# A two-layer hybrid block (attention, convolution, Fourier) on one core: the Fourier gate's projection moved beside attention, and the first scale and shift used piece by piece for eight token tiles

## The chip, the core and the metric

The kernel runs on one core of a Trainium2 chip. The metric is the device time of one execution in microseconds (us). Before the change three runs gave a median of 1203.3 us (1202.12 to 1205.43).

## The reference, cut to what matters

Two layers over 1024 latent and 256 context tokens of width 1024. Each layer: a norm with scale and shift that come from a conditioning vector (adaLN), one wide projection whose columns feed three branches and their gates, and an output projection over the gated branches.

```python
for l in range(2):
    shift, scale, gate = split(silu(c) @ w_ada[l] + b_ada[l])        # and the same with c_ctx
    hc = rms_norm(h_ctx, norm_g[l]) * (1 + scale_c) + shift_c        # context
    hx = rms_norm(x, norm_g[l]) * (1 + scale) + shift                # latent
    # columns: q 512, k 128, v 128, g_att 512, c_a 256, c_b 256, g_conv 256, f_u 256, g_four 256
    px = split_cols(hx @ w_in[l])
    attn = windowed_attention(rope(q), rope(k), v, kc, vc, sink)     # +-128 tokens, and all of the context
    y_conv = silu(layer_norm(depthwise_conv31(c_a * sigmoid(c_b))))
    y_four = Re(fft2(f_u)) @ w_four + b_four
    y = concat([attn * silu(g_att), y_conv * silu(g_conv), y_four * silu(g_four)]) @ w_out[l]
    x = x + gate * y       # in layer 0 the context stream goes the same way
return rms_norm(x, final_g)
```

In layer 1 the context only gives keys and values.

## The kernel before

**Precision.** Every float32 matmul operand is held as two parts, hi and lo (`hxh`, `hxl` for the modulated input, `wh`, `wl` for weights), and each product is three matmuls (`mm3`, lines 195 to 197 in the profile). One column tile of the projection (128 columns, `C_GF`, `C_Q` and so on name the first) over one chunk of tokens is 8 blocks of the inner width times 3, so 24 matmuls into one PSUM bank. Layer 0 has three chunks (512 and 512 latent, 256 context), layer 1 two, and three for the keys and values.

**Order of the work.** The program is recorded call by call. A scheduler then places the instructions of each engine in a fixed order, by its own simulated timeline and a priority number that rises as the program is recorded (`tc.cur_priority`). So the order in which the code calls things shapes the order on each engine, without setting it alone. On the chip each engine runs its list in order and waits at semaphores.

**Startup.** `load_x` fetches a tile of 128 tokens; `first_norm` divides it by its root mean square (VectorE and GpSimd in turn). The scale and shift columns of layer 0 come in four pieces `u` of two column blocks each: `ada_load` (4 transfers of 512 KB), `ada_sums` (line 285, matmuls over `wada`), `ada_cols` (line 300, selector matmuls, then four small VectorE operations). `transposes` (line 380) turns normed tokens, and `modulate` (lines 393 and 396) applies scale and shift and makes `hxh` and `hxl`. `Pair` projects two column tiles, those of the Fourier input, chunk by chunk: `p0` for tokens 0 to 511, which follows the pieces; `p1` for tokens 512 to 1023; `p2` for the context.

**A layer.** The *projection stage* runs through `todo` by `projections`, a chunk at a time into the banks `mm` and `pt` in turn (`mmx`): both convolution inputs, then the two tiles of the Fourier gate (`C_GF`), keys, values, queries. Between chunks it advances `side()` (the Fourier transform `four`, gate rows, layer 1's scale and shift) and `fill_v(budget)`, which records some of the 31 taps of the convolution (`conv_taps`) on VectorE, as a background that `Behind` keeps behind other work. The gate of `C_GF` is finished by `gf_evac`: a tanh on ScalarE (line 514) and two products on VectorE (`t<-t,mm`, then `F<-F,t`).

*Attention* follows: `Attention`, 40 steps in layer 0 and 32 in layer 1, each for one block of 128 queries and two heads: scores (lines 893 and 895), softmax on VectorE, ScalarE and GpSimd, transposes (949), values (963). Between two steps PE is given one chunk from `rest()`: the attention gate (`C_GATT`), `conv_norm` (576, 594), the convolution gate (`C_GC`), then halves of the output projection (`OP`). The kernel's tail is the last output tiles and the final norm.

## Time and profile before

| what | value |
| --- | --- |
| median of 3 runs | 1203.3 us |
| the profiled execution | 1202.68 us, its span 1200.6 us |
| mean granted TensorE clock | 0.964 of full speed |
| TensorE (PE) busy | 1103.3 us, 92% of the span |
| VectorE (DVE) busy | 820.6 us, 68% |
| ScalarE (ACT) busy | 554.7 us, 46% |
| GpSimd (POOL) busy | 295.0 us, 25% |
| chain that ended last | PE 70%, DVE 10%, DMA 9%, ACT 4% |

The span is the time from the first to the last instruction that the profiler saw; 2.08 us of the execution lie outside it. Busy shares are means over stages with different limits: PE is nearly full in both projection stages, and has gaps in the startup, in both attentions and in the tail.

### The profile page before, as it was taken

The page shows a single profiled execution, that of the slowest core. Times are in us where ns is not written, and L with a number is a line of the kernel's source. Part 1 is how long each engine was busy: PE and PEld are TensorE (multiplying, and loading weights), DVE is VectorE, ACT ScalarE, POOL GpSimd, SP SyncE. Part 2 cuts the span into 40 slices and gives each one's busy share as a digit, 9 for nine tenths or more (in the row PEclk, how much of TensorE's full clock was granted, in tenths as well). Part 3 has the DMA queues.
Part 4 walks back from the last instruction along what each step waited for, and adds up shares of the span by engine and source line. Part 5 has one row for each costly group of instructions (what it writes and reads, how often), then busy time and mean ns, then how long its engine had stood idle before and what let it go on. Part 6 is the DMA issues. An engine that isn't in the chain of part 4 may idle for free.

```text
span 1200.6 us, 17131 instructions
## 1 busy us (share of the span) xinstructions
PE 1103.3 (92%) x6165; PEld 925.9 (77%) x6165; DVE 820.6 (68%) x1665; ACT 554.7 (46%) x1209; POOL 295.0 (25%) x266
## 2 busy tenths in 40 slices
PE   5799999999999989999889999999989979988866
PEld 3488887888888878888668788788778868877754
DVE  3425879999577786666755369889656786766654
ACT  5563222312566655564646652222255654545541
POOL 1212000000222443544342120000022453334321
PEclk9799999999999999999979999999989989999889
DMA  9602273744332433544436423532243453322221
GB/s 332 218 25 71 70 239 113 225 137 108 84 97 75 149 115 102 166 142 132 115 120 227 145 65 116 184 110 79 88 93 106 136 145 103 110 74 71 71 71 53
DMA packets 154093, 146.49 MB, mean 122 GB/s; under 512 B 7398, under 2 KB 131734, under 8 KB 154008
## 3 DMA queue, kind: packets, MB, share of 16 engines
q1 hardware_dynamic: 154008, 145.40, 39.5%
q8 instruction: 49, 0.80, 0.3%
q14 instruction: 36, 0.29, 0.1%
HBM read 110.49 MB, written 34.87 MB: 121 GB/s over the span
## 4 chain that ended last, share of the span: by engine, by line
PE 70%; DVE 10%; DMA 9%; ACT 4%; issue 3%; SPq 2%; POOL 1%; DVEq 0%; ACTq 0%; POOLq 0%
PE mm L195 13%; PE mm L197 13%; PE mm L196 13%; PE pt L195 5%; PE pt L196 5%; PE pt L197 5%; PE mm L963 4%; PE pt L949 4%; DMA od<-ot 3%; PE score L893 2%; DVE score L57 2%; DVE pl L57 2%; PE score L895 2%; DMA wr<-od 1%; ACT p L919 1%
## 5 line engine op out<-in xcount | busy, mean ns | idle before, releaser
L195 PE MATMUL mm<-hxh,wh 128*128 128x512 f32 (+1 forms) x808 | 311.5, 386 | 5.5 <-DVE t L57 3.2
L197 PE MATMUL mm<-hxh,wl 128*128 128x512 f32 (+1 forms) x808 | 306.7, 380 | 2.4 <-POOL wl L405 2.3
L196 PE MATMUL mm<-hxl,wh 128*128 128x512 f32 (+1 forms) x808 | 307.4, 380 | 0.0
L195 PEld LDWEIGHTS mm<-hxh,wh 128*128 128x128 f32 x808 | 153.8, 190 | 37.5 <-DVE t L57 4.3
L57 DVE SCALAR_TENSOR_TENSOR cy<-cu,cw,cy 128x1014 f32<-128x1014 f32 (+20 forms) x180 | 180.1, 1007 | 2.6
L197 PEld LDWEIGHTS mm<-hxh,wl 128*128 128x128 f32 x808 | 153.6, 190 | 30.3 <-POOL wl L405 3.1
L935 POOL TENSOR_SCALAR p<-p,st 128x640 f32<-128x640 f32 (+2 forms) x144 | 114.4, 809 | 249.1 <-DVE st L57 129.1
L196 PEld LDWEIGHTS mm<-hxl,wh 128*128 128x128 f32 x808 | 154.0, 191 | 25.0 <-issue 0.5
L405 POOL TENSOR_TENSOR wl<-wr,wh 128x1024 fp32r<-128x1024 f32 x26 | 64.2, 2468 | 396.3 <-ACT wh L404 394.1
L954 ACT ACTIVATE ph<-pt 128x512 fp32r<-128x512 f32 x184 | 97.4, 542 | 121.0 <-PE pt L949 118.2
L57 DVE TENSOR_TENSOR pl<-pt,ph 128x512 fp32r<-128x512 f32 x184 | 112.3, 616 | 57.8 <-ACT ph L954 56.4
L949 PE MATMUL pt<-ident,p 128*128 128x128 f32 x640 | 107.6, 286 | 24.5 <-DVE pl L57 19.1
L919 ACT ACTIVATE p<-score,st 128x640 f32<-128x640 f32 (+2 forms) x144 | 105.3, 734 | 36.5 <-DVE st L57 29.2
L57 DVE CUSTOM_DVE_ANT_0 score<-score,mask,nsink 128x640 f32<-128x640 f32 (+2 forms) x144 | 110.8, 782 | 13.8 <-PE score L895 13.0
L195 PE MATMUL pt<-hxh,wh 128*128 128x512 f32 (+1 forms) x296 | 112.2, 383 | 3.9 <-ACT hxh L393 2.5
L404 ACT ACTIVATE wh<-wr 128x1024 fp32r<-128x1024 f32 x56 | 59.7, 1066 | 116.5 <-PE mm L196 73.1
L196 PE MATMUL pt<-hxl,wh 128*128 128x512 f32 (+1 forms) x296 | 111.1, 376 | 0.7 <-DVE hxl L57 0.7
L197 PE MATMUL pt<-hxh,wl 128*128 128x512 f32 (+1 forms) x296 | 110.4, 373 | 0.9 <-DVE wl L57 0.9
L949 PEld LDWEIGHTS pt<-ident,p 128*128 128x128 f32 x640 | 79.8, 146 | 38.2 <-POOL p L935 8.7
L963 PE MATMUL mm<-ph,v 128*128 128x256 f32 x320 | 93.1, 314 | 13.2 <-ACT ph L954 10.7
L963 PE MATMUL mm<-pl,v 128*128 128x256 f32 x320 | 93.7, 315 | 5.3 <-DVE pl L57 4.9
L963 PEld LDWEIGHTS mm<-ph,v 128*128 128x128 f32 x320 | 64.6, 202 | 18.3 <-ACT ph L954 15.8
(220 smaller groups left out, 1797.8 us busy)
## 6 DMA issues: line engine op xcount, KB each, us to landing
wada<-w_ada SPq DMA_DIRECT2D x48, 512.0 KB, 7.0
wr<-w_in SPq DMA_DIRECT2D x38, 512.0 KB, 4.1
qq<-qd SPq DMA_DIRECT2D x36, 256.0 KB, 4.3
x1d<-x SPq DMA_DIRECT2D x10, 512.0 KB, 3.0
xnd<-xr SPq DMA_DIRECT2D x10, 512.0 KB, 3.7
p<-xnd SPq DMA_DIRECT2D x10, 512.0 KB, 4.8
sg<-sgd SPq DMA_DIRECT2D x36, 128.0 KB, 3.0
od<-ot SPq DMA_DIRECT2D x18, 256.0 KB, 2.5
```

Source lines behind the costliest of these rows:

```text
L57: r = f(*args, **kw)
L195: T.matmul(o, lhsT=lhs[0], rhs=rhs[0], start=start, stop=False)
L196: T.matmul(o, lhsT=lhs[0], rhs=rhs[1], start=False, stop=False)
L197: T.matmul(o, lhsT=lhs[1], rhs=rhs[0], start=False, stop=stop)
L404: S.activation(hi, raw, AF.Copy)
L405: (E or (G if holding[0] else V)).tensor_tensor(out=lo, in0=raw, in1=f32(hi), op=ALU.subtract)
L893: T.matmul(sc[:, c0:512], lhsT=q2[:, h, :], rhs=kx[:, k0:k0 + nl], start=fst, stop=not fst)
L919: S.activation(pp[:, j * n:(j + 1) * n], z["sc"][j][:, 768 - n:768], AF.Exp, scale=-1.0, bias=st[:, j:j + 1], accum_out=st[:, 4 + j:5 + j])
L935: G.tensor_scalar(out=pp[:, j * n:(j + 1) * n], in0=pp[:, j * n:(j + 1) * n], scalar1=st[:, 6 + j:7 + j], scalar2=1.0, op0=ALU.mult, op1=A ...
L949: T.transpose(out=bt[:, (j % 2 * 2 + y) * P:(j % 2 * 2 + y + 1) * P], in_=pp[:, c0:c0 + P], identity=ident)
L954: S.activation(ph, bt[:, :w], AF.Copy)
L963: T.matmul(o, lhsT=self.vv[kt][:, kv * P:(kv + 1) * P], rhs=y.cols(j * 256, (j + 1) * 256), start=(j == 0 and x == 0), stop=(j == z["nkt"] ...
```

## The change

It has five parts. First, the tiles of `C_GF` go from the projection stage to the front of attention's fillers, ahead of `C_GATT`, in the bank `mm`; the call that drained the Fourier transform inside `gf_evac` goes; the rope tables are loaded at the stage's third chunk; `side()` advances twice a chunk towards the stage's end; the budgets of taps rise from 3.0 and 5.0 to 4.0 and 6.0. Second, the taps are recorded with a priority number 300 higher, and in layer 0 the context's taps come ahead of the latent ones. Third, at the start each piece `u` of the scale and shift modulates tokens 0 to 511 and 512 to 1023 in turn, `p0` and `p1` advance step by step beside each other, and the loop that did `p1` afterwards goes. Fourth, for that the x tiles 4 to 7 are loaded ahead of the second piece of `wada`, and `ada_sums` and `ada_cols` use halves of a `score` bank. Fifth, in layer 0 `modulate` reads PSUM with one activation into `q`, and VectorE copies `q` to the hi part; before, two activations did that.

```diff
     def fill_v(us):
+        p0 = tc.cur_priority
+        tc.cur_priority = p0 + 300
         V.background = True
...
         V.background = False
+        tc.cur_priority = p0
...
             hi, lo = hx[k][0].cols(t0, t0 + n), hx[k][1].cols(t0, t0 + n)
-            for o in (hi, q):
+            for o in (q, hi)[:1 if l == 0 else 2]:
                 S.activation(o, two[:, j * n:(j + 1) * n], AF.Identity, scale=ada_col(1, st, k),
                              bias=ada_col(0, st, k))
+            if l == 0:
+                V.tensor_copy(out=hi, in_=q)
             E = G if k % 4 == 3 else V
...
                                    in1=z.cols(o0, o1), op0=ALU.mult, op1=ALU.add)
-        for s0, s1 in spans:
+        for s0, s1 in spans[::-1]:
             us = 1.25 if s0 == 0 else 0.4
...
                     back.append((us, lambda a=(s0, s1, j): tap(*a)))
-        back.append((0.0, u.put))
+            back.append((0.0, u.put_ctx if s0 else u.put_lat))
...
     wa = w_begin(0, C_FU)
-    z[1] = ada_load(1)
     first_norm(groups[0], (V, G))
...
     wb = w_tile_short(0, C_FU + P)
+    for t in groups[1]:
+        load_x(t)
+    z[1] = ada_load(1)
     pair = [wa, wb]
-    p0 = Pair(pair, 0, (pt, pt))
+    p0, p1 = Pair(pair, 0, (pt, pt)), Pair(pair, 1, (mm, mm))
     for u in range(4):
...
         alloc_hx(two)
-        tr = transposes(groups[0], xs, two)
-        t = ada_sums(z[u], mm)
+        sc = score()
+        banks = iter((sc[:, 0:512], sc[:, 512:1024]))
+        part = ada_sums(z[u], lambda: next(banks))
         if u < 2:
             z[u + 2] = ada_load(u + 2)
+        if u == 1:
+            for t in groups[2]:
+                load_x(t)
+        tr = transposes(groups[0], xs, two)
+        ada_cols(0, u, part, lambda: sc)
+        modulate(0, groups[0], tr, two)
         if u:
-            p0.step([2 * u - 2, 2 * u - 1])
-        ada_cols(0, u, t, mm)
-        modulate(0, groups[0], tr, two)
-        if u == 1:
-            for t in groups[1]:
-                load_x(t)
+            p1.step([2 * u - 2, 2 * u - 1])
+        if u in (0, 2):
+            first_norm(groups[1 + u // 2], (V, G))
+        tr = transposes(groups[1], xs, two)
+        p0.step(two)
+        modulate(0, groups[1], tr, two)
     for i in raws:
         i.put()
-    for t in groups[2]:
-        load_x(t)
     wc = w_split(w_begin(0, C_B))
-    p0.step([6, 7])
-    for t in groups[0]:
+    for t in groups[0] + groups[1]:
         xs[t].put()
...
     p0.end(ev0)
-    first_norm(groups[1], (V, G))
+    p1.step([6, 7])
+    p1.end(ev0)
...
     project(wc, 0, evb, pt)
-    first_norm(groups[2], (V, G))
-    p1 = Pair(pair, 1, (mm, mm))
-    for i in range(5):
-        two = [2 * i, 2 * i + 1]
-        if i < 4:
-            tr = transposes(groups[1], xs, two)
-        if i:
-            p1.step([2 * i - 2, 2 * i - 1])
-        if i < 4:
-            modulate(0, groups[1], tr, two)
-    p1.end(ev0)
     cr = conv_load()
...
         modulate(0, groups[2], tr[i], range(4 * i, 4 * i + 4))
-    for t in groups[1] + groups[2]:
+    for t in groups[2]:
         xs[t].put()
...
             yield from four
-            tab.extend(bufs.get("rope") for _ in range(2))
-            for i, name in enumerate(("k_cos", "k_sin")):
-                nc.sync.dma_start(out=tab[i].lat, in_=a[name])
             gsum = bufs.get("gsum")
...
             def f(o, c0, c1):
-                drain(four)
                 gate_mul(F[m], 0.5, yd[256 + m * P:256 + (m + 1) * P, :])(o, c0, c1)
...
                 (C_A + P, full, glu_a(1, wctx), lambda: taps(1), mmx)]
-        for m in range(2):
-            todo.append((C_GF + m * P, full) + gf_evac(m) + (mmx,))
         k_at = sum(len(t[1]) for t in todo) + 3
...
         q_at = sum(len(t[1]) for t in todo)
-        budget = [(3.0 if t[0] < C_V else 5.0) * (0.5 if c == 2 else 1.0) for t in todo for c in t[1]]
+        budget = [(4.0 if t[0] < C_V else 6.0) * (0.5 if c == 2 else 1.0) for t in todo for c in t[1]]
+        for m in range(2):
+            todo.append((C_GF + m * P, full) + gf_evac(m) + (mm,))
         for j in range(4):
...
             c = next(pj)
+            if i == 2:
+                tab.extend(bufs.get("rope") for _ in range(2))
+                for t, name in zip(tab, ("k_cos", "k_sin")):
+                    nc.sync.dma_start(out=t.lat, in_=a[name])
             steps(sd)
+            if i >= k_at - 3:
+                steps(sd)
             if i >= k_at:
...
             for i, c in enumerate(pj):
-                if i == 4 * len(full) - 2:
+                if i == 6 * len(full) - 2:
                     raw = w_begin(l, C_GC)
-                if i == 4 * len(full) - 1:
+                if i == 6 * len(full) - 1:
                     box.append(w_split(raw))
...
                     steps(cn)
```

On PE in the startup, before: `L285` sums the last piece of `wada`, `pt` takes `p0`, `L300` makes the last columns, and the first matmul of `p1` (into `mm`, from `hxh_186`) stands behind it.

```order
87 L380 MATMUL score<-ident,x_326 128x128
88 L285 MATMUL mm<-wada_117,s2p 32x256 x4
89 L196 MATMUL pt<-hxl_334,wh 128x512
90 L197 MATMUL pt<-hxh_332,wl 128x512
91 L196 MATMUL pt<-hxl_334,wh_172 128x512
92 L197 MATMUL pt<-hxh_332,wl_174 128x512
93 L300 MATMUL mm<-sel,t_414 128x2 x4
94 L195 MATMUL mm<-hxh_186,wh 128x512
95 L195 MATMUL mm<-hxh_186,wh_160 128x512
96 L195 MATMUL pt<-hxh_397,wh 128x512
97 L195 MATMUL pt<-hxh_397,wh_178 128x512
```

After, where `L288` and `L383` are the sums and transposes: `p1`'s first matmuls (`mm<-hxh_196`) stand ahead of transposes and of sums over the second piece (`wada_116`, `wada_117`).

```order
37 L198 MATMUL mm<-hxh_196,wh 128x512
38 L198 MATMUL mm<-hxh_196,wh_156 128x512
39 L383 MATMUL score<-ident,x_88 128x128
40 L383 MATMUL score<-ident,x_90 128x128
41 L383 MATMUL score<-ident,x_108 128x128
42 L383 MATMUL score<-ident,x_110 128x128
43 L383 MATMUL score<-ident,x_88 128x128
44 L383 MATMUL score<-ident,x_90 128x128
45 L383 MATMUL score<-ident,x_108 128x128
46 L383 MATMUL score<-ident,x_110 128x128
47 L288 MATMUL score<-wada_116,s2p 32x256 x4
48 L288 MATMUL score<-wada_117,s2p 32x256 x4
```

So `p1` moved from behind the four pieces to between them. The DVE list in layer 1 at the end of the projection stage, before: the last tap (`cy_7131<-cu_7093`), the rope of the last queries (`STREAM_SHUFFLE`, `rope`), the values' lo parts (`v`), and at once the subtraction of the convolution's mean from `mm`.

```order
1114 L57 SCALAR_TENSOR_TENSOR cy_7131<-cu_7093,cw,cy_7131 128x1010
1115 L57 TENSOR_TENSOR q_434_7862<-q_434_7862,rope_7271 128x512
1116 L57 TENSOR_TENSOR t_7913<-t_7913,rope_7272 128x512
1117 L57 TENSOR_TENSOR v_7871<-pt,v_7871 128x2x64
1118 L57 TENSOR_TENSOR v_7870<-pt,v_7870 128x2x64
1119 L57 SCALAR_TENSOR_TENSOR cy_7131<-cu_7093,cw,cy_7131 128x1009
1120 L57 TENSOR_TENSOR q_434_7862<-q_434_7862,t_7913 128x512
1121 L57 TENSOR_TENSOR v_7871<-pt,v_7871 128x2x64 x2
1122 L57 TENSOR_TENSOR cy_6890<-cy_6890,mm 128x512
1123 L57 TENSOR_TENSOR cy_7131<-cy_7131,mm 128x512
1124 L57 STREAM_SHUFFLE t_7965<-q_439_7963 128x512
1125 L57 STREAM_SHUFFLE t_8007<-q_439_7963 128x512
```

After, at the same place:

```order
1126 L57 TENSOR_TENSOR q_434_7722<-q_434_7722,t_7773 128x512
1127 L57 TENSOR_TENSOR v_7731<-pt,v_7731 128x2x64
1128 L57 SCALAR_TENSOR_TENSOR cy_7131<-cu_7092,cw,cy_7131 128x1015
1129 L57 TENSOR_TENSOR v_7731<-pt,v_7731 128x2x64
1130 L57 SCALAR_TENSOR_TENSOR cy_7131<-cu_7092,cw,cy_7131 128x1014
1131 L57 SCALAR_TENSOR_TENSOR cy_7131<-cu_7092,cw,cy_7131 128x1013
1132 L57 SCALAR_TENSOR_TENSOR cy_7131<-cu_7092,cw,cy_7131 128x1012
1133 L57 SCALAR_TENSOR_TENSOR cy_7131<-cu_7092,cw,cy_7131 128x1011
1134 L57 SCALAR_TENSOR_TENSOR cy_7131<-cu_7092,cw,cy_7131 128x1010
1135 L57 SCALAR_TENSOR_TENSOR cy_7131<-cu_7092,cw,cy_7131 128x1009
1136 L57 STREAM_SHUFFLE t_7825<-q_439_7823 128x512
1137 L57 STREAM_SHUFFLE t_7867<-q_439_7823 128x512
```

The taps now end in a run of six behind the third query tile's last rope addition (`q_434`, row 1126), ahead of the last query tile's shuffles (`q_439`). On PE in attention of layer 1, before: two steps' scores (`L893`, `L895`) stand four transposes apart, with no chunk of 24 matmuls between them.

```order
4395 L895 MATMUL score<-kd_7638,q_463_8644 128x256
4396 L893 MATMUL score<-kh_7639,q_463_8644 128x384
4397 L893 MATMUL score<-kd_7637,q_463_8644 128x384
4398 L895 MATMUL score<-kh_7640,q_463_8644 128x256
4399 L895 MATMUL score<-kd_7638,q_463_8644 128x256
4400 L949 MATMUL pt<-ident,p_8982 128x128 x4
4401 L893 MATMUL score<-kh_7595,q_485_9042 128x384
4402 L893 MATMUL score<-kd_7593,q_485_9042 128x384
4403 L895 MATMUL score<-kh_7596,q_485_9042 128x256
4404 L895 MATMUL score<-kd_7594,q_485_9042 128x256
4405 L963 MATMUL mm<-ph_8995,v_7870 128x256
4406 L963 MATMUL mm<-pl_8997,v_7870 128x256
```

After, a little further on in the same attention: the scores of a step, and the first matmuls of a projection chunk (`L198` to `L200`) right behind them. `L954` and `L968` are the transposes and values.

```order
4322 L968 MATMUL mm<-pl_8852,v_7733 128x256
4323 L898 MATMUL score<-kh_7439,q_482_8896 128x384
4324 L898 MATMUL score<-kd_7437,q_482_8896 128x384
4325 L900 MATMUL score<-kh_7440,q_482_8896 128x256
4326 L900 MATMUL score<-kd_7438,q_482_8896 128x256
4327 L198 MATMUL mm<-hxh_6162,wh 128x512
4328 L199 MATMUL mm<-hxl_6164,wh 128x512
4329 L200 MATMUL mm<-hxh_6162,wl 128x512
4330 L198 MATMUL mm<-hxh_6166,wh 128x512
4331 L199 MATMUL mm<-hxl_6168,wh 128x512
4332 L200 MATMUL mm<-hxh_6166,wl 128x512
```

Layer 1's attention has 22 such chunks after the change against 18 before, layer 0's four wide and two half-wide ones more.

## Rows read from the trace of the kernel before

**Rows 1.** The page, busy time of each engine, its share and instructions.

```profile
PE 1103.3 (92%) x6165; PEld 925.9 (77%) x6165; DVE 820.6 (68%) x1665; ACT 554.7 (46%) x1209; POOL 295.0 (25%) x266
```

**Rows 2.** Windows: stretch, length, busy of PE, PEld, DVE, ACT, POOL (instructions), granted clock, DMA share, GB/s.

```profile
0.00:34.00 34.00, 20.40 (x145) 12.87 (x145) 11.58 (x43) 19.57 (x35) 4.94 (x8) 1.00 1.01 338
...
34.00:60.40 26.40, 19.56 (x113) 11.41 (x111) 13.00 (x43) 12.92 (x21) 6.10 (x4) 0.74 0.63 189
...
102.50:302.30 199.80, 199.80 (x1196) 165.35 (x1195) 171.43 (x263) 49.65 (x92) 2.95 (x1) 1.00 0.48 145
...
302.30:558.00 255.70, 246.75 (x1489) 217.82 (x1488) 177.78 (x419) 151.55 (x355) 101.88 (x91) 0.99 0.38 115
...
558.00:602.00 44.00, 37.86 (x213) 31.70 (x212) 31.50 (x101) 25.74 (x70) 16.41 (x20) 0.93 0.42 123
...
922.00:1149.00 227.00, 200.23 (x1132) 173.76 (x1130) 159.47 (x362) 124.48 (x291) 89.21 (x76) 0.95 0.35 102
```

**Rows 3.** Timeline, 30 to 40 us, and the page's DMA issues: start, length, engine, line, operation.

```profile
32.41 1.06 ACT L1180 ACTIVATE p<-x 128x1024 f32<-128x1024 f32 x1 [0.19 <-DMA x<-x]
...
35.83 3.20 POOL L1183 TENSOR_SCALAR x<-x,ry 128x1024 f32<-128x1024 f32 x2 [3.31 <-DVE ry L57]
...
wada<-w_ada SPq DMA_DIRECT2D x48, 512.0 KB, 7.0
```

**Rows 4.** Timeline of PE, one chunk of 24 matmuls and what follows it.

```profile
303.68 0.40 PE L195 MATMUL mm<-hxh,wh 128*128 128x512 f32 x1
...
309.14 1.88 PE L576 MATMUL mm<-cy,onesm 128*128 128x512 f32 x4
```

**Rows 5.** Windows of DVE: stretch, length, busy (instructions).

```profile
118.70:302.30 183.60, 164.66 (x251) 1.00 0.49 149
722.00:852.90 130.90, 119.12 (x139) 1.00 0.38 118
```

**Rows 6.** Waits (us, times, longest), then lines by shape, DVE, 118.7 to 302.3 us.

```profile
DVE t L57 <- ACT t L514: 4.8, 4, 1.8
...
L57 DVE TENSOR_TENSOR wl<-wr,wh 128x1024 fp32r<-128x1024 f32 x9 | 11.0, 1221 | 0.7 <-ACT wh L404 0.7
...
L57 DVE SCALAR_TENSOR_TENSOR F<-F,t 128x512 f32<-128x512 f32 x4 | 2.8, 688 | 0.1
...
L57 DVE SCALAR_TENSOR_TENSOR t<-t,mm 128x512 f32<-128x512 f32 x4 | 2.8, 688 | 3.2 <-ACT t L514 3.0 <-ACT t L501 0.2
...
L57 DVE SCALAR_TENSOR_TENSOR F<-F,t 128x256 f32<-128x256 f32 x2 | 0.8, 420 | 0.0
```

**Rows 7.** Timeline of PE, first score matmuls of four steps in layer 1's attention.

```profile
931.05 0.34 PE L893 MATMUL score<-kh,q 128*128 128x384 f32 x1
...
940.04 0.34 PE L893 MATMUL score<-kh,q 128*128 128x384 f32 x1
...
991.58 0.44 PE L893 MATMUL score<-kh,q 128*128 128x384 f32 x1 [1.21 <-ACT p L919]
...
1008.02 0.34 PE L893 MATMUL score<-kh,q 128*128 128x384 f32 x1
```

**Rows 8.** Timeline at the end of layer 1's projection stage.

```profile
860.21 1.02 PE L576 MATMUL mm<-cy,onesm 128*128 128x512 f32 x2
...
861.27 1.28 DVE L57 TENSOR_TENSOR cy<-cy,mm 128x512 f32<-128x512 f32 x2 [8.39 <-PE mm L576]
...
877.45 0.38 PE L893 MATMUL score<-kh,q 128*128 128x256 f32 x1
```

**Rows 9.** Timeline of two copies on DVE, alone and beside GpSimd.

```profile
409.02 0.43 DVE L57 CAST hxh<-wor 128x512 fp32r<-128x512 f32 x1
...
444.83 1.29 POOL L405 TENSOR_TENSOR hxl<-wor,hxh 128x512 fp32r<-128x512 f32 x1 [1.82 <-ACT hxh L404]
...
444.86 1.53 DVE L57 CAST hxh<-wor 128x512 fp32r<-128x512 f32 x1
```

## The prediction

> **What bounds the kernel now.** First the page: PE is busy 92% of the span, DVE 68% [rows 1]. So the time is PE's work plus the places where PE waits or runs at a lower clock, and the windows show where these are [rows 2]. In layer 0's projection stage (102.5 to 302.3 us) PE is busy all of the 199.8 us: whatever leaves that stage is a gain there, unless DVE, busy 171.4 of it, becomes the bound. In attention of layer 0 PE lacks 9.0 us of 255.7, and 6.1 of the next 44, there at a clock of 0.93. In attention of layer 1 it lacks 26.8 of 227. In the startup the first 34 us go by the load (DMA share 1.01, 338 GB/s); in the 26.4 after them PE is idle for 6.8 us and runs at 0.74 for the other 19.56, which at full clock would be 14.5: 12 us are there to be had at most.
>
> Next come PE's own rows. A chunk of 24 matmuls takes from 303.68 to 309.14, so 5.46 us [rows 4]; a half-wide chunk I take as 2.73. In layer 1's attention a step with a chunk takes 940.04 − 931.05 = 8.99 us, and such steps have almost no gap: 5.46 for the chunk and 3.53 for the step's own matmuls. The two steps from 991.58 to 1008.02 have two chunks and still take 16.44 [rows 7], near their dense 17.98. The gaps come with steps that have no chunk: their PE work is 3.5 us, and the chain scores, maximum, exponential, divide, transpose is longer than that.
>
> **The change, part by part.**
>
> *Fourier gate in layer 0.* Two column tiles leave a full PE stage: 4 × 5.46 + 2 × 2.73 = 27.3 us. Whether the stage shrinks by all of it depends on DVE. From the first tap to the stage's end (118.7 to 302.3, 183.6 us) DVE is busy 164.7 [rows 5]. With the chunks go eight products of about 0.69 us and four half-wide ones of about 0.42, 7.2 in all, and two of the nine splits `wl` of 1.22 each [rows 6], since the tiles' weights are now split beside attention: 164.7 − 7.2 − 2.4 = 155.1. PE's work there is 183.6 − 27.3 = 156.3. So DVE, at 155.1 plus what it waits, is as long as PE. It idled 18.9 us; 4.8 of that were waits for the gate's tanh [rows 6], which go too. If none of the other 14.1 remained, nothing is lost; if all of it did, 155.1 + 14.1 − 156.3 = 13. The taps now give way to other work (priority) and more are offered per chunk (budgets), so DVE should seldom be without work; nothing in these rows times that. I take 3 of 0 to 13.
>
> *The same in attention.* The 27.3 us of PE work come back there, and what counts is how much falls into gaps. By the order, eight steps of layer 0 had no chunk of their own; now it is six, and the last ten steps, where four were empty, all have one. There the gap is 6.1 us, and 37.86 us of work at 0.93 cost another 2.7 [rows 2]. I take 7: the gap and a part of the clock. Bounds: 3, half the gap, and 14, nearly all 15.1 of both windows.
>
> *Layer 1.* Here 4 × 5.46 = 21.8 us move. DVE from 722.0 to 852.9 is busy 119.1 of 130.9 [rows 5]; without eight products (5.5) and two splits (2.4) 111.2. The convolution's second mean, at 860.21, needs the last tap; DVE had waited 8.39 us for it and attention starts at 877.45 [rows 8]. With 21.8 us less PE would be at the mean at 838.4, so DVE has 116.4 us from 722.0 for 111.2 and its waits, 0 to 10.7 after the tanh's: a stall of 0 to 5.5. The run of six taps ahead of the last query tile's rope also delays the first queries, by up to 6 × 1.27. I take 3, the middle. In attention 25 steps lie between 922 and 1149, with 18 chunks: 18 × 5.46 + 25 × 3.53 = 186.5, so 40.5 of the 227 are lost to gaps and clock, in ten empty steps: 4.05 each. After, five are empty. At layer 0's price (15.1 us over eight empty steps, 1.9 each) five filled steps save 9.5, at layer 1's 20; I take 15, since a filled step draws some of its wait with it.
>
> *Startup.* The four x tiles go ahead of five transfers of 512 KB [rows 3], at 338 GB/s 1.55 us each: they land 7.8 us earlier. The last arrived at 32.41 and was normed at 39.03 [rows 3]; now about 31.3, and `p1`'s matmuls can fill gaps from about 33. That is worth up to the 12 us above. Against it: the second piece of `wada` lands 6.2 us later (four tiles of 512 KB), so that PE will have done some 6 us less by 34. And the eight tiles take turns in two `score` banks, which now also hold the sums: three times a chain (columns on DVE, activation, copy, subtraction, matmul) ends bare: the added copy of 0.43 us [rows 9], a subtraction of about 0.69, as the products of that size [rows 6], and small column operations, some 1.3 us each and 4 in all. The activation that goes lay beside the subtraction's wait and gives nothing back here. 12 − 6 − 4 = 2 us gained, between −4 (the tiles early, the gaps not filled) and +8 (no bubble, a part of the clock).
>
> The copies total forty, some 15 us of DVE in the startup, where it is busy 13.0 of 26.4 [rows 2]; nothing else needs it there. But the copy at 444.86, which began beside a GpSimd operation of 1.29 us, took 1.53 instead of 0.43 [rows 9]. Every fourth block's subtraction is GpSimd's, so four copies that meet one would cost 4 × 1.1 = 4.4 us; the sum goes by none, since GpSimd is busy 6.1 of those 26.4 us. The Trainium skill, in "SBUF — State Buffer", section "Who interferes with whom", says that a cast on DVE can need a port pair shared with GpSimd, an exclusive lock, and that the one that comes second blocks until the first is done. By that rule, with which the trace agrees for this one pair, the startup would gain nothing and the time be 1189.
>
> The rest: the context's taps ahead of the latent ones and the earlier rope tables are neutral for PE, as the same 62 taps must be done by the mean. The loads of the gate convolution's weights start two chunks per tile later but in the same place of the fillers. The tail is unchanged.
>
> **Sum:** startup 2, layer 0 27.3 − 3 − (27.3 − 7) = 4, layer 1 21.8 − 3 − (21.8 − 15) = 12, together 18. From the profiled execution's 1202.7 us (its span 1200.6 and 2.1 around it) that gives 1184.7, so **1185**; the median of the runs is 0.6 higher, and I take no account of that.
>
> **The rivals.** *A, slower:* the moved chunks are paid in full in attention. PE works in order, so a chunk laid between two steps delays the next scores, and the chain behind them is as long as before; the gaps then stay and the chunks come on top. Saving 0 instead of 22, the sum is 2 − 6 = −4, so 1207. For it speak the empty steps' long price, which might be a latency that a chunk merely shifts; against it the dense steps of 8.99 us without gaps. It decides if less than 4 of the 22 are saved. *B:* DVE bounds both projection stages with its waits kept, stalls 13 and 5.5 instead of 3 and 3: 1185 + 12.5 = 1197. For it speak 155.1 against 156.3; against it that taps can run at any time. *C:* the copies meet GpSimd, 4.4 us, in the startup's bare chain: 1189. *D, better:* attention's bounds and the startup's all at the good end and no stall: 8 + 14 + 20 = 42, which can hardly all happen at once; with 8 in the startup, 20 in layer 1, 7 in layer 0 and 3 of stall it is 32, so 1170. For it speaks the size of the gaps in layer 1, against it that a chunk can't lie in all of a gap.
>
> **How the numbers follow.** Chances: the likeliest .50, with its own range 1177 to 1194; A .10; B .15; C .10; D .15. What a measurement of this kernel can tell from no change is 0.3%, 3.6 us: faster means below 1199.7, slower above 1206.9. A lies at that upper bound, so .06 of it goes to slower and .04 to same; B with the startup at its bad end too reaches 1203 and beyond, .04 for each; slower .10, same .08, and the rest, .82, faster. The range leaves A out and half of D, not 2 in 10, and holds B: 1170 to 1202.
>
> **What would show it.** Right: the projection stage of layer 0 about 24 us shorter, with PE busy nearly all of it and DVE above 95%; layer 0's attention some 20 us longer with the gap at its end gone; layer 1's projection stage 19 shorter, its attention 7 longer with PE lacking about 15 instead of 26.8; `p1` done with the pieces, PE at a clock well over 0.74 between 34 and 60 us. Wrong: a PE wait for `cy` (line 576 of before) or for `cu` in the projection stages (B); scores that start later after each chunk, steps of 12 us with one chunk (A); copies of 1.5 us beside GpSimd with PE waiting behind (C); or PE's first `mm` matmuls waiting for x tiles still, which would take the startup's gain away.

## The result: half a per cent slower

Eight runs of the changed kernel have a median of 1209.4 us against 1202.7 for eight of the kernel before: ratio 1.0055, 95% interval 1.0035 to 1.0075. The prediction, 1185, had the wrong sign. Single runs of one kernel spread over some 10 us here, so every ratio below comes with its interval. The profiled execution after took 1211.5 us, with this page (the lines that answer to [rows 1]):

```profile
span 1209.3 us, 17169 instructions
...
PE 1102.7 (91%) x6165; PEld 924.8 (76%) x6165; DVE 837.2 (69%) x1685; ACT 542.2 (45%) x1185; POOL 299.6 (25%) x270
```

PE's work is the same to 0.6 us (1103.3 before). The span is 8.7 us longer, so PE's idle time grew by 9.3. Where, the windows tell, cut at four events that both traces have: the first convolution input of layer 0 (first `cu` on DVE), its first score, and the same two of layer 1. So the five stretches are the startup, layer 0's projection stage, its attention with the way into layer 1, layer 1's projection stage, its attention with the tail. Columns as in [rows 2]. Before:

```profile
0.00:102.50 102.50, 82.07 (x491) 60.67 (x492) 40.04 (x112) 58.93 (x103) 23.54 (x22) 0.93 0.54 173
102.50:302.30 199.80, 199.80 (x1196) 165.35 (x1195) 171.43 (x263) 49.65 (x92) 2.95 (x1) 1.00 0.48 145
302.30:705.90 403.60, 381.49 (x2153) 329.24 (x2152) 260.19 (x633) 240.56 (x563) 151.38 (x144) 0.97 0.40 125
705.90:877.40 171.50, 170.03 (x849) 137.79 (x847) 139.41 (x175) 44.09 (x76) 7.31 (x4) 1.00 0.38 116
877.40:1200.60 323.20, 269.94 (x1481) 232.82 (x1481) 209.54 (x485) 161.50 (x375) 109.81 (x96) 0.93 0.31 92
```

After:

```profile
0.00:101.90 101.90, 79.91 (x490) 59.75 (x491) 48.19 (x135) 43.69 (x78) 23.93 (x22) 0.95 0.57 185
101.90:287.60 185.70, 175.85 (x1050) 141.22 (x1048) 154.25 (x240) 44.64 (x82) 0.08 (x1) 0.98 0.45 134
287.60:718.40 430.80, 405.03 (x2297) 352.47 (x2298) 283.88 (x654) 246.28 (x574) 157.41 (x147) 0.97 0.42 125
718.40:870.30 151.90, 148.98 (x754) 119.76 (x752) 133.69 (x168) 41.19 (x71) 7.26 (x4) 1.00 0.39 114
870.30:1209.30 339.00, 292.97 (x1578) 251.63 (x1577) 217.22 (x491) 166.35 (x381) 110.97 (x98) 0.93 0.31 93
```

Layer 0's stage, full before, now has 9.9 us in which PE stands and a granted clock of 0.98. It shrank by 14.1 us where 27.3 us of work had left. DVE has room: it is busy for 154.3 us of 185.7. The attentions got longer by 27.2 of the 27.3 us of work that they were given, and by 15.8 of 21.8. What PE waited for in layer 0's stage is in the chain of waits (total us, times, longest):

```profile
PE pt L361 <- ACT kh L409: 5.3, 1, 5.3
PE mm L288 <- DMA wada<-w_ada: 3.0, 3, 1.4
PE pt L288 <- DMA wada<-w_ada: 0.7, 1, 0.7
```

L361 makes the gate rows from `gsum`; L288 sums over ada weights, first those of the gate rows, then layer 1's. Both belong to `side()`, the side work that the change steps twice a chunk. In the timeline of this place the bias row that the gate rows need is issued by SP at 190.25, between loads for the keys, and PE goes on at 195.09:

```profile
189.11 1.10 SPq L1355 DMA_DIRECT2D kd<-kd  x2
...
190.25 0.44 SPq L349 DMA_DIRECT2D gsum<-b_ada  x1
191.74 4.51 SPq L1355 DMA_DIRECT2D kd<-kd  x4
193.98 1.06 ACT L409 ACTIVATE kh<-kd 128x1024 fp32r<-128x1024 f32 x1 [3.56 <-DMA kd<-kd]
...
195.09 1.19 PE L361 MATMUL pt<-gsum,sel 128*128 128x512 f32 x1 [5.31 <-ACT kh L409]
```

The view names the ACT operation that ended at about the same moment, but that makes key parts, which L361 doesn't read. What L361 reads is `gsum`, and in the run e4 below, with the same wait, the view names the bias row's transfer. By the loop, two chunks lie between the last sum into `gsum` and the gate rows when the side work is stepped once a chunk, and one when it is stepped twice.

The wait also costs clock. PE stood from 189.8 to 195.1 us, and from 192 to 198 its granted clock is 0.50 of full speed, the lower of its two levels (1.2 GHz); the first gate-row matmul takes 1.19 us, where before the change the same one takes 0.59:

```profile
192.00:198.00 6.00, 2.91 (x5) 1.40 (x5) 2.79 (x3) 1.06 (x1) 0.00 (x0) 0.50 0.91 229
```

So of the 13.2 us that the stage lost, 9.9 are PE's idle time, and the other 3 or so are slower work: PE is busy 175.9 us with what was to take 199.8 − 27.3 = 172.5.

At the entry to layer 0's attention, the timeline after shows a second new wait:

```profile
287.52 2.37 POOL L410 TENSOR_TENSOR wl<-wr,wh 128x1024 fp32r<-128x1024 f32 x1 [192.29 <-ACT wh L409]
287.65 3.31 DVE L57 SCALAR_TENSOR_TENSOR cy<-cu,cw,cy 128x1010 f32<-128x1010 f32 x1
...
292.36 0.68 DVE L57 SCALAR_TENSOR_TENSOR t<-t,mm 128x512 f32<-128x512 f32 x1
...
293.08 0.80 PE L198 MATMUL mm<-hxh,wh 128*128 128x512 f32 x1 [4.21 <-DVE t L57]
293.63 1.26 DVE L57 SCALAR_TENSOR_TENSOR cy<-cu,cw,cy 128x1009 f32<-128x1009 f32 x1
```

The convolution's taps are not done when attention begins at 287.67; the last starts at 293.63. The product that empties the first filler's bank (`t<-t,mm`) stands behind the tap before that one, and PE waits 4.21 us for the bank.

### The profile page after: what moved, and what is told of

Same layout as the page of the kernel before. It is cut to its first block, busy times and chain, and to the rows that moved or that the text cites. A ratio compares the mean times of both kernels' runs of the same rounds, so it can differ in the third digit from the quotient of the medians.

```text
span 1209.3 us, 17169 instructions
## 1 busy us (share of the span) xinstructions
PE 1102.7 (91%) x6165; PEld 924.8 (76%) x6165; DVE 837.2 (69%) x1685; ACT 542.2 (45%) x1185; POOL 299.6 (25%) x270
## 4 chain that ended last, share of the span: by engine, by line
PE 61%; DVE 14%; DMA 12%; issue 4%; ACT 4%; SPq 2%; POOL 2%; DVEq 0%; ACTq 0%; POOLq 0%
PE mm L198 11%; PE mm L199 11%; PE mm L200 11%; PE pt L198 4%; PE pt L954 4%; PE pt L200 4%; PE mm L968 4%; PE pt L199 4%; DMA wr<-od 3%; DVE cy L57 2%; PE score L898 2%; DVE score L57 2%; PE score L900 2%; DMA wada<-w_ada 1%; DVE pl L57 1%
## 5 line engine op out<-in xcount | busy, mean ns | idle before, releaser
L198 PE MATMUL mm<-hxh,wh 128*128 128x512 f32 (+1 forms) x832 | 318.4, 384 | 16.4 <-DVE t L57 11.2
L199 PE MATMUL mm<-hxl,wh 128*128 128x512 f32 (+1 forms) x832 | 314.8, 378 | 0.0
L200 PE MATMUL mm<-hxh,wl 128*128 128x512 f32 (+1 forms) x832 | 314.4, 378 | 0.0
L198 PEld LDWEIGHTS mm<-hxh,wh 128*128 128x128 f32 x832 | 159.0, 191 | 47.5 <-DVE t L57 13.5
L57 DVE SCALAR_TENSOR_TENSOR cy<-cu,cw,cy 128x1009 f32<-128x1009 f32 (+23 forms) x180 | 179.8, 1018 | 1.9
L200 PEld LDWEIGHTS mm<-hxh,wl 128*128 128x128 f32 x832 | 158.7, 191 | 28.2 <-issue 0.8
L199 PEld LDWEIGHTS mm<-hxl,wh 128*128 128x128 f32 x832 | 159.1, 191 | 27.1 <-issue 2.8
L410 POOL TENSOR_TENSOR wl<-wr,wh 128x1024 fp32r<-128x1024 f32 x30 | 71.5, 2384 | 378.4 <-ACT wh L409 378.4
L954 PE MATMUL pt<-ident,p 128*128 128x128 f32 x640 | 104.7, 283 | 14.4 <-DVE pl L57 12.5
L198 PE MATMUL pt<-hxh,wh 128*128 128x512 f32 (+1 forms) x272 | 105.3, 392 | 6.9 <-DVE hxh L57 4.8
L200 PE MATMUL pt<-hxh,wl 128*128 128x512 f32 (+1 forms) x272 | 103.2, 379 | 0.9 <-DVE wl L57 0.9
L968 PE MATMUL mm<-ph,v 128*128 128x256 f32 x320 | 91.5, 310 | 13.6 <-ACT ph L959 6.1
L199 PE MATMUL pt<-hxl,wh 128*128 128x512 f32 (+1 forms) x272 | 103.1, 380 | 0.0
L954 PEld LDWEIGHTS pt<-ident,p 128*128 128x128 f32 x640 | 78.6, 145 | 26.8 <-DVE pl L57 8.3
L968 PE MATMUL mm<-pl,v 128*128 128x256 f32 x320 | 92.3, 311 | 2.9 <-DVE pl L57 2.9
L968 PEld LDWEIGHTS mm<-ph,v 128*128 128x128 f32 x320 | 63.8, 199 | 17.3 <-ACT ph L959 8.1
```

Source lines behind the costliest of these rows:

```text
L57: r = f(*args, **kw)
L198: T.matmul(o, lhsT=lhs[0], rhs=rhs[0], start=start, stop=False)
L199: T.matmul(o, lhsT=lhs[0], rhs=rhs[1], start=False, stop=False)
L200: T.matmul(o, lhsT=lhs[1], rhs=rhs[0], start=False, stop=stop)
L410: (E or (G if holding[0] else V)).tensor_tensor(out=lo, in0=raw, in1=f32(hi), op=ALU.subtract)
L954: T.transpose(out=bt[:, (j % 2 * 2 + y) * P:(j % 2 * 2 + y + 1) * P], in_=pp[:, c0:c0 + P], identity=ident)
```

## The experiments

A table first. It gives the ratio to the kernel before with its interval, and the lengths of the five stretches in the profiled execution, which lies anywhere in a kernel's spread (so differences under some 5 us in one stretch say little alone: layer 0's code is the same in e5 and e9, and its stage takes 175.5 and 179.4). In e1, e4 and e6 one chunk fewer runs ahead of layer 1's first score than in the other kernels without the move there, which makes their stage 1 some 5.5 us shorter and their attention 1 as much longer.

| kernel | ratio (95%) | startup | stage 0 | attention 0 | stage 1 | attention 1, tail |
| --- | --- | --- | --- | --- | --- | --- |
| before | 1 | 102.5 | 199.8 | 403.6 | 171.5 | 323.1 |
| after | 1.0055 (1.0035 to 1.0075) | 101.9 | 185.8 | 430.8 | 151.9 | 339.0 |
| e1 no move | 1.0048 (1.0027 to 1.0069) | 99.8 | 206.4 | 409.6 | 167.1 | 320.0 |
| e2 move only | 1.0061 (1.0039 to 1.0084) | 100.1 | 185.3 | 428.9 | 151.8 | 335.4 |
| e3 move in layer 1 | 1.0047 (1.0026 to 1.0068) | 101.2 | 206.5 | 407.8 | 153.2 | 332.4 |
| e4 move in layer 0 | 1.0039 (1.0018 to 1.0059) | 100.2 | 188.4 | 432.2 | 167.0 | 316.7 |
| e5 side work late | 0.9969 (0.9950 to 0.9988) | 99.9 | 175.5 | 423.7 | 159.1 | 332.4 |
| e6 no move, side once | 0.9971 (0.9954 to 0.9987) | 100.7 | 199.8 | 410.1 | 166.2 | 319.0 |
| e7 two activations | 1.0090 (1.0066 to 1.0113) | 104.8 | 192.6 | 430.8 | 153.2 | 333.4 |
| e8 startup only | 1.0019 (1.0003 to 1.0034) | 101.6 | 199.8 | 408.1 | 171.8 | 322.1 |
| e9 side late in layer 0, once in 1 | 0.9944 (0.9919 to 0.9969) | 100.5 | 179.4 | 424.8 | 154.4 | 334.4 |
| e10 e9, light gate | 0.9686 (0.9661 to 0.9710) | 100.5 | 182.9 | 407.8 | 151.8 | 319.8 |
| e11 before, side twice | 1.0024 (1.0008 to 1.0041) | 100.1 | 205.7 | 404.5 | 173.8 | 315.5 |
| e12 e9, old startup | 0.9938 (0.9911 to 0.9964) | 101.9 | 177.4 | 420.3 | 156.0 | 335.4 |
| e13 e9, no lo output weights | 0.9867 (0.9847 to 0.9887) | 102.8 | 177.8 | 424.6 | 156.0 | 320.8 |
| e14 e12, layer 1 hurried | 0.9920 (0.9893 to 0.9946) | 100.5 | 179.0 | 421.6 | 151.6 | 333.4 |

One part needed no run: the taps' priority number. With its lines taken out, the built program has the same instructions in the same order. It does nothing.

**e1 to e4: which part loses.** e1 puts the chunks back (the diff, from the changed kernel); e3 and e4 do so in one layer; e2 is the kernel before with only the move and what the change did to the projection stage.

```diff
+        for m in range(2):
+            todo.append((C_GF + m * P, full) + gf_evac(m) + (mmx,))
         k_at = sum(len(t[1]) for t in todo) + 3
...
-        for m in range(2):
-            todo.append((C_GF + m * P, full) + gf_evac(m) + (mm,))
```

> The changed kernel with the Fourier gate's chunks put back in the projection stage of both layers (startup by pieces, copies, priority of the taps, order of spans and budgets kept). Theory 1, the move itself is what costs (the chunks leave 33.7 us of the two stages and come back as 43.0 in the attentions): ratio to before 0.997 to 1.002, as the startup alone is 0.6 us shorter. Rival, the move is worth its 18 us and the other parts (priority of the taps, copies on VectorE) cost 25: ratio 1.015 or more.

> The kernel before with only the move of the Fourier gate's chunks, with its budgets, the second step of the side work, the early rope tables and the context's taps first (which the move needs for its buffers); startup, copies and priority as before. Theory 1: ratio 1.004 to 1.010, as the whole change. Rival, the other parts undo what the move gains: ratio 0.98 to 0.99.

> The changed kernel with the move in layer 1 alone. By the stages of the two traces layer 1 gained 19.6 in its projection stage and gave back 15.8 in attention and tail, so 3.8 us in all: ratio 0.994 to 0.999 if the layers add up. Rival, the loss sits at the end of layer 1 (its attention and tail 15.8 us longer whatever layer 0 does) and its stage gain needs layer 0's change: ratio 1.003 or more.

> The changed kernel with the move in layer 0 alone. By the stages layer 0 gained 14.1 in its projection stage and gave back 27.2 by the first convolution input of layer 1, so it loses 13 us: ratio 1.009 to 1.012 if the layers add up. Rival, layer 0's move is neutral and the two layers' losses come from the taps' priority: ratio 0.998 to 1.003.

All four are 0.4 to 0.6% slower than before. Neither the first theory (the move costs it) nor its rival (the other parts do) stands: e1 loses without the move, e2 without startup, copies and priority, and the layers don't add up. What all five slow kernels share is the stage's new rules: the second side step, the budgets, the early rope tables, the order of the taps. Layer 0's stage takes 206 us without the move, where before it took 199.8. The waits of e4 name the place:

```profile
PE pt L361 <- DMA gsum<-b_ada: 6.8, 1, 6.8
PE mm L288 <- DMA wada<-w_ada: 3.8, 5, 2.4
```

**e5: the side work stepped twice only late.** With the move there are 27 chunks in layer 0's stage, and the side work ends in its 18th: it is done 9 chunks early.

```diff
-            if i >= k_at - 3:
+            if i >= k_at + 4:
                 steps(sd)
```

> The changed kernel with the side work stepped twice a chunk only from the stage's 17th chunk on in layer 0 (14th in layer 1) instead of from the tenth (7th). Theory 2, the hurried side work stalls PE in layer 0's projection stage, since the gate rows and the sums over the ada weights now come right behind the issue of their transfers: PE's wait of 5.3 us before the gate rows and most of its 3.7 for the ada weights go, the stage is 7 to 12 us shorter, ratio to before 0.996 to 1.001. Rival, the lost 13 us are VectorE's (the prediction's rival B): ratio 1.004 to 1.007, stage as long as now.

0.9969: one number in the code takes 0.9% off and turns the sign. Layer 0's stage and attention in its windows:

```profile
99.85:275.30 175.45, 174.17 (x1052) 141.30 (x1050) 153.96 (x242) 43.90 (x82) 0.00 (x0) 1.00 0.48 142
275.30:699.00 423.70, 402.41 (x2296) 351.21 (x2296) 280.37 (x651) 246.22 (x575) 156.93 (x147) 0.98 0.42 127
```

The stage is 24.3 us shorter than before with PE idle for 1.3. DVE is as busy as after (154.0), so the rival, a stage bound by DVE, falls.

**e9: once a chunk in layer 1.** In e5 the wait had come up in layer 1, where its second steps now fell on the gate rows (2.0 us) and the ada sums (3.6).

```diff
-            if i >= k_at - 3:
+            if i >= k_at + 4 and not last:
                 steps(sd)
```

> The changed kernel with the second side step only in layer 0 and only from the 17th chunk on; layer 1 steps once a chunk. In the run with both layers late, layer 1's projection stage waited 3.6 us for ada weights and 2.0 for the gate's bias row, just where its second steps began. Theory 2: these go too, layer 1's stage is back at about 152 us, ratio 0.990 to 0.995. Rival, the waits are those of the transfers themselves and stay whatever the steps: ratio 0.996 to 0.999.

0.9944, in theory 2's range (the interval reaches the rival's). Layer 1's stage fell from 159.1 to 154.4, not to 152: the wait for ada weights went, that of 2.0 us for the bias row stayed, though the side work is stepped once. As the change has it, stepped twice from earlier on, that wait is 0.4 us. So in layer 1 it is the place of the steps that makes this wait, not their number. Against the changed kernel e9 is 1.1% faster, some 13 us. Layer 0's taps now end in time, the last ones of 1.27 us each from 271.38, while attention begins at 279.85:

```profile
271.38 2.58 DVE L57 SCALAR_TENSOR_TENSOR cy<-cu,cw,cy 128x1010 f32<-128x1010 f32 x2
```

and the wait at attention's entry is gone. Its first 22 us, of e9:

```profile
279.85:301.85 22.00, 21.89 (x141) 19.27 (x142) 18.54 (x40) 13.26 (x35) 7.73 (x6) 1.00 0.21 67
```

and of the changed kernel:

```profile
287.60:309.60 22.00, 17.18 (x86) 13.83 (x87) 17.18 (x32) 9.40 (x24) 5.02 (x5) 0.84 0.18 61
```

So the hurried side work cost twice: PE stood behind its transfers, and DVE, whose list had small operations on the ada columns in the same place, stood behind PE, so that the taps ran late into attention. DVE's waits for those columns from 170 us to attention, after:

```profile
DVE ada L57 <- PE pt L303: 5.3, 2, 5.1
```

and in e9:

```profile
DVE ada L57 <- PE pt L303: 0.3, 1, 0.3
```

**e11: the second side step alone,** in the kernel before (`if i >= k_at - 3: steps(sd)` added to it).

> The kernel before with nothing but the second side step from three chunks before the keys on. Theory 2: the hurry alone stalls PE in layer 0's projection stage, whose 199.8 us become 204 to 209, ratio 1.003 to 1.007. Rival, the stall needs the shorter stage or the new startup: stage at 200 us, ratio 0.998 to 1.002.

The stage is 5.9 us longer, as expected, the whole 1.0024, just under the range given:

```profile
100.12:305.86 205.74, 202.91 (x1196) 165.78 (x1195) 169.46 (x258) 50.28 (x92) 2.81 (x1) 0.99 0.47 141
```

PE is idle for 2.8 us of it, all for ada weights; the other 3.1 are the same matmuls as before in more time (202.9 us for 199.8), with a granted clock of 0.99 for 1.00. A part of the cost is there without the other edits. With them it is larger: 0.8% between e1 and e6 below, which differ in the second step alone, and 0.9% between the changed kernel and e5, which takes it later.

**e6 and e8: what is left without the move.** e6 is e1 without the second side step (the diff); e8 is the kernel before with the new startup, the copies and the priority.

```diff
-            if i >= k_at - 3:
-                steps(sd)
```

> The changed kernel without the move in either layer and with the side work stepped once a chunk throughout, as before. By theory 2 most of what the version without the move lost came from the second step: ratio 0.996 to 1.001, layer 0's projection stage back from 206 to about 200 us. Rival, the startup by pieces or its copies cost it: ratio 1.003 to 1.007, with the 206 us kept.

> The kernel before with only the startup by pieces for all eight latent tiles, the copies and the taps' priority number (which moves no row). By the first inputs of the convolution, which come at 100.2 to 101.9 us in five traces against 102.5, the startup is worth 0 to 2 us: ratio 0.997 to 1.000. Rival, the startup's order upsets what follows: ratio 1.003 or more.

e6: 0.9971, its layer 0 stage at 199.8 again. e8: 1.0019, between the two ranges, its interval just above 1: the startup is no gain. From e8 to e6 the only edits are the budgets, the early rope tables and the context's taps first, and they are worth about 0.5%; the prediction called the latter two neutral and costed the first at nothing by itself. Which of the three does it is not settled. By the table they work in layer 1, whose stage and attention together take 485.2 us in e6 and 493.9 in e8. And e6 against e9 (0.9971, 0.9944) is the move, with the side work late in layer 0: 0.3%, by overlapping intervals. By the single profiles what it gains lies in layer 0, whose stage and attention take 597.7 to 604.2 us in e5, e9, e12 and e14, and 603.4 to 609.9 without the move (before, e8, e6). In layer 1 the four take 485.0 to 491.5, so as long as e6 or longer. Layer 1 of e6:

```profile
710.70:876.80 166.10, 164.56 (x826) 133.51 (x824) 138.27 (x173) 43.70 (x74) 5.11 (x4) 1.00 0.39 116
876.80:1195.80 319.00, 271.34 (x1505) 233.77 (x1505) 208.77 (x488) 162.57 (x379) 115.96 (x97) 0.94 0.31 93
```

**e7 and e12: the copies and the startup.** e7 is the changed kernel with the two activations of before (the diff); e12 is e9 with the whole startup of before.

```diff
-            for o in (q, hi)[:1 if l == 0 else 2]:
+            for o in (hi, q):
...
-            if l == 0:
-                V.tensor_copy(out=hi, in_=q)
```

> The changed kernel with the hi part of the modulated input written by a second activation in layer 0, as before, instead of by a copy on VectorE. If the copies that meet GpSimd cost time in the startup (the prediction's rival C), the startup is 2 to 4 us shorter and the ratio 1.001 to 1.004; if they lie beside other work, nothing moves: ratio 1.004 to 1.007.

> As the first of these four, but with the startup of before: the second x tiles late, one group of tokens after the other, two activations for the hi and the full part. The prediction's 2 us for the startup by pieces would make this 0.002 slower than the first of these; if the startup is worth nothing, no difference; the copies' cost (rival C) would make it faster by 0.002 to 0.004.

e7 is slower, 1.0090, above both ranges, its startup 2.9 us longer and its layer 0 stage 6.8: nothing is won back by taking the copies out. Why the stage is longer too is open, and the interval overlaps that of the changed kernel. e12 and e9 are alike (0.9938, 0.9944): the startup by pieces is worth nothing that these runs can tell. In the five traces with the old startup it ends at 100.1 to 102.5 us, in ten with the new one and its copies at 99.8 to 102.8.

**e10: what a chunk in attention costs.** e9 with 8 of 24 matmuls in each of the moved chunks (the light gate).

```diff
         for k in range(NK):
+            if one:
+                T.matmul(o, lhsT=wh[:, ks], rhs=hx[k][0].cols(c0, c1), start=k == 0, stop=k == NK - 1)
+                continue
             mm3(o, (wh[:, ks], wl[:, ks]), (hx[k][0].cols(c0, c1), hx[k][1].cols(c0, c1)), k == 0, k == NK - 1)
```

> The same kernel, with the Fourier gate's projection from the hi parts alone: 8 of the 24 matmuls of each of its ten chunks, so that two thirds of 49.1 us of PE work, 32.7 us, are left out of the attentions. If a chunk laid in attention is paid in full there (the prediction's rival A), the time falls by 28 to 33 us against the same kernel with all matmuls, ratio to before 0.963 to 0.970; if chunks fill gaps as the prediction's sum had it (22 of 49 us saved), by about 18, ratio 0.975 to 0.980.

0.9944 to 0.9686: 2.6% of 1201 us, 31 us for 32.7 us of matmuls, or 27 to 35 by the two intervals. A filler chunk is paid in full or nearly so. That is what rival A said of attention. The run shortens the chunks and does not take them away, and in layer 1 three of the four run ahead of the first score.

**e13: why the gaps don't fill.** In the changed kernel, a gap in layer 1's attention looks like this:

```profile
986.08 4.81 POOL L410 TENSOR_TENSOR hxl<-wor,hxh 128x512 fp32r<-128x512 f32 x3
986.58 1.51 DVE L57 CAST hxh<-wor 128x512 fp32r<-128x512 f32 x1
...
988.47 1.30 DVE L57 TENSOR_TENSOR hxl<-wor,hxh 128x512 fp32r<-128x512 f32 x1
...
989.69 1.49 DVE L57 CAST hxh<-wor 128x512 fp32r<-128x512 f32 x1
...
991.10 0.88 DVE L57 CUSTOM_DVE_ANT_0 score<-score,mask,nsink 128x640 f32<-128x640 f32 x1
...
992.07 0.80 ACT L924 ACTIVATE p<-score,st 128x640 f32<-128x640 f32 x1 [4.64 <-DVE st L57]
...
993.01 0.45 PE L898 MATMUL score<-kh,q 128*128 128x384 f32 x1 [2.98 <-ACT p L924]
```

The output weights (`wor`) are split into hi and lo on DVE, ScalarE and GpSimd, the maximum of the scores (`score<-score,mask,nsink`) stands behind that on DVE, the exponential behind the maximum, and PE behind the exponential, since it needs the score bank. The kernel keeps the split weights in the buffers of `hxh` and `hxl`, so that the burst can't begin until the last projection chunk is done. More chunks push it later (in layer 1 it begins at 951.1 us before and 981.7 after, 74 and 111 us behind the first score); they don't take it away. e13 takes its subtractions away:

```diff
-            split(self.hi[k].lat[:, hs], self.lo[k].lat[:, hs], self.raw[h, k], V if k % 2 else G, k % 2 == 1)
+            if k % 2:
+                V.tensor_copy(out=self.hi[k].lat[:, hs], in_=self.raw[h, k])
+            else:
+                S.activation(self.hi[k].lat[:, hs], self.raw[h, k], AF.Copy)
...
-                mm3(o, (yh[:, ks], yl[:, ks]), (self.wo.hi[k][:, hs], self.wo.lo[k][:, hs]), k == 0, k == NK - 1)
+                mm3(o, (yh[:, ks], yl[:, ks]), (self.wo.hi[k][:, hs], self.wo.hi[k][:, hs]), k == 0, k == NK - 1)
```

> The kernel of e9 with the lo parts of the output weights left out: the 32 subtractions that make them go (half on VectorE, half on GpSimd), and the third matmul of each output product reads the hi part in their place, so that PE's work stays. Theory 3, the gaps of attention sit where the output weights are split in a burst on VectorE, ScalarE and GpSimd, which delays the softmax: PE's idle time in attention falls by 5 us or more, ratio to before 0.984 to 0.990 (the kernel of e9 had 0.9944). Rival, the gaps are the softmax chain's own: idle time as in e9, ratio 0.992 to 0.997.

0.9867. Layer 1's attention and tail, e9 and then e13:

```profile
859.00:1193.40 334.40, 291.19 (x1577) 249.00 (x1577) 214.98 (x491) 166.50 (x381) 112.75 (x98) 0.94 0.31 95
```

```profile
861.20:1182.00 320.80, 286.75 (x1577) 246.44 (x1577) 206.09 (x483) 165.15 (x381) 101.15 (x90) 0.95 0.33 99
```

With as many matmuls, PE's idle time falls from 43.2 to 34.1 us, and the stretch by 13.6. So the burst makes part of layer 1's gaps. In layer 0 nothing changed (424.8 and 424.6), and 34 us remain in layer 1, about half of them in the tail: theory 3 holds for layer 1, and for a part.

**e14: the best version.** e12 with layer 1's side work as the change has it (twice from three chunks before the keys), layer 0's late.

```diff
-            if i >= k_at + 4 and not last:
+            if i >= (k_at - 3 if last else k_at + 4):
                 steps(sd)
```

> The kernel of e12 (startup of before), with layer 1's side work hurried as in the change (that stage took 151.8 to 151.9 us hurried, 154.4 to 156.0 stepped once). By the stages 2.5 to 4 us better than e12: ratio 0.990 to 0.993. Rival, layer 1's side work makes no difference: 0.992 to 0.996.

0.9920 (0.9893 to 0.9946), in both ranges, median 1189.3 us: faster than both kernels. Layer 1's stage is at 151.6, where the change as made had waited only 0.4 us for the bias row. The intervals of e9, e12 and e14 overlap, so that this last step is shown by its stretch (156.0 to 151.6; 151.8 to 153.2 in the other kernels that hurry there), not by the whole.

## Why the prediction was wrong, step by step

Two steps failed. The one that turned the sign is the second step of the side work: it has no term in the sum. The prediction spoke of the rope tables as neutral; `side()` advancing twice it didn't price at all, although several of its steps issue transfers that a later one reads, and stepping twice halves the work between. Against e5 and e9 it cost 6 to 10 us in layer 0's stage and, by the late taps, 6 to 7 more in its attention. Repaired (e5, e9), the kernel is faster than before, but by 4 to 7 us and not by 18. The step that failed there is layer 1's gain of 12, with its 15 us saved in attention: the move gains nothing in layer 1 that the profiles show.

- **Layer 0's stage, 27.3 − 3.** With the change as made it shrank by 14.1: the term for the second step was missing. In e5 it shrank by 24.3, the very sum, in e9, e12, e13 and e14 by 20.4 to 22.4. But the 3 us were to be DVE's, and that is not what they are: from the first tap on DVE was to be busy for 155.1 of 156.3 us, and was for 148.5 of 163.2 in e5 (148.8 of 173.5 after); what PE waits for in that stage of e5 and of e9 is ada weights, not taps. So the size is right by luck. Rival B's 13 us came, but not by its cause. From the first tap on, e5:

```profile
112.10:275.30 163.20, 161.92 (x974) 130.13 (x973) 148.51 (x232) 40.69 (x78) 0.00 (x0) 1.00 0.51 150
```

- **Layer 0's attention, 7 us saved.** After: 0.1. In e5: 27.3 − 20.1 = 7.2, in e9 6.1. So the size was right, once the taps end in time, but filled gaps are not what the traces show: PE is idle there for 21.3 us in e5 and 22.4 in e9, against 22.1 before. What is less is PE's busy time for the same work, at a granted clock of 0.98 for 0.97; how much of it is the clock is open.
- **Layer 1's stage, 21.8 − 3.** After the change it shrank by 19.6 against 18.8: right. The stall of 2.5 us at 855.66 is about the 3, but not the one foreseen: the last tap ends at 851.4, ahead of the mean at 852.11, and PE waits for a filler's bank, behind DVE's wait of 2.0 us for the last queries.
- **Layer 1's attention, 15 us saved.** After: 6.0. In e5, e9 and e14 it is 12.5, 10.5 and 11.5 against the kernel before. But e6, without any move, is 4.1 us shorter than before with a chunk more in the stretch (x1505 for x1481), so that 9.6 of that come without the move. Against e6 three more chunks (x1577, 16.4 us) lengthen it by 13.4, 15.4 and 14.4: 1 to 3 us saved, by single profiles. The step "40.5 us are lost to gaps and clock, in ten empty steps: 4.05 each" failed: the gaps were put down to steps without a chunk, because they stood beside such steps in the list. e13 shows that 9 us of PE's idle time go with the output weights' subtractions.
- **Startup, 2 us.** 0.6 by the trace, nothing by e8 and by e9 against e12. The clock did rise where the prediction looked, from 0.74 to 0.94 between 34 and 60 us, but the first 34 us lost it again: PE was busy for 14.95 us of them against 20.40.

```profile
0.00:34.00 34.00, 14.95 (x85) 8.01 (x85) 15.14 (x50) 15.97 (x29) 6.79 (x9) 0.90 1.01 336
34.00:60.40 26.40, 24.54 (x170) 17.87 (x170) 15.93 (x45) 10.64 (x19) 5.21 (x3) 0.94 0.62 192
```

- **Rival A** came near the time (1207 against 1209.4) by half a reason and luck: chunks are paid nearly in full (e10), but the second step's cost, which it didn't have either, makes up most of the loss.
- **Rival C** came in a part that costs nothing: there are 24 copies (11.8 us, not forty and 15), and three of them took 1.13 to 1.51 us instead of 0.28 to 0.43 (at 43.72, 45.51 and 70.69 us), but PE shows no wait of over 0.25 us behind them. e7 agrees.

The sum had 18 us; the best version of this change (e14) has about 10, by 0.8% of 1201, and 14 in its profile, and some 3.5 of that e6 has without the move.

## What to carry to other kernels

When a loop that interleaves side work gets shorter, don't only raise the steps per turn: count, for each step, what transfers it issues and how much work lies between their issue and their use. Price every edit of the list, the small ones too. An instruction that waits on an in-order engine delays also what other engines have queued behind its result, so look for the second wait one stage later. Gaps beside unfilled steps are not proof that filling will close them: first see which engine's queue the released instruction stood in, and what stood ahead of it. And when a stretch is cut at an event, compare the counts of matmuls before the lengths: an event can come a chunk earlier.

## What the runs showed of the hardware that was not expected

A DVE operation with two inputs in SBUF that begins beside a GpSimd split of weights takes as long as that still needs, and nearly its own time after. After the change a tap of 1.27 us took 3.31 (287.65 to 290.96), begun 0.13 us into a split of 2.37 us that ended at 289.89: from there it is 1.07 us. In e1 an addition took 2.76 us, begun at 303.71 beside a split from 303.45 to 305.93, so 0.54 us from there; such operations of 128 x 512 take 0.68 alone:

```profile
303.45 2.48 POOL L410 TENSOR_TENSOR wl<-wr,wh 128x1024 fp32r<-128x1024 f32 x1 [210.34 <-ACT wh L409]
303.71 2.76 DVE L57 TENSOR_TENSOR q<-q,t 128x512 f32<-128x512 f32 x1
```

The trace after has 42 such meetings with a GpSimd operation of two inputs. Each took the rest of GpSimd's and then its own shortest time, less 0.03 to 0.18 us. The prediction had looked for this with the copies alone [rows 9]. The Trainium skill, "SBUF — State Buffer", section "Who interferes with whom", says that DVE with two SBUF inputs contends with GpSimd's reads too and that the second one blocks until the first is done; these two rows agree with that.
